# Rotary tables scaled once per layer, projection results copied out by ScalarE, rotary products on VectorE; earlier norm squares and first score blocks set wider apart, in a two-layer fp32 trunk

## The chip, the core and the metric

The kernel runs on one core of one Trainium2 chip. The metric is the device time of one execution, in microseconds (us). Five engines work side by side, each with its own queue that it runs in order: PE (TensorE, matmuls and transposes), DVE (VectorE), ACT (ScalarE), POOL (GpSimd) and SP (SyncE, which here only starts transfers).

## The reference, cut to what matters

512 tokens, model width 2048, two layers. Of one layer:

```python
h = rms_norm(x, pre_norm_g[l])                       # x * rsqrt(mean(x*x) + eps) * g
proj = einsum('bsd,de->bse', h, w_in[l])             # 2048 -> 6656 columns
rq, rk, rv, rg, dq, dk, dv, dg, lx, lg = split(proj) # 768 x4, 512 x4, 768 x2
ret  = rms_norm(retention(rope(rq), rope(rk), rv)) * silu(rg)       # 6 heads of 128
diff = rms_norm(diff_attention(rope(dq), rope(dk), dv)) * silu(dg)  # 4 heads, two softmaxes each
lru  = rg_lru(lx) * silu(lg)                         # convolution, two gates, a scan over time
y = einsum('bse,ed->bsd', concat([ret, diff, lru]), w_out[l])
x = x + rms_norm(y, post_norm_g[l])

def rope(x, positions, inv_freq):
    ang = positions[..., None] * inv_freq
    cos, sin = cos(ang)[:, :, None, :], sin(ang)[:, :, None, :]
    x1, x2 = split(x, 2, axis=-1)
    return concatenate([x1 * cos - x2 * sin, x2 * cos + x1 * sin], axis=-1)
```

All in fp32. The factor rsqrt(mean(x*x) + eps), below rstd, is one number for each token. The kernel leaves it out of the matmul's input and multiplies it into the results of the projection.

## The kernel before, in words

**The matmuls.** A layer is a list of passes: 13 over the input projection (512 columns each), then 5 over the output projection. A pass sums 16 blocks of 128 rows of the contraction into four PSUM banks, the tiles `big`. For fp32 accuracy each product is three matmuls on a high and a low part (`whi`, `wlo` of the weights, `hhi`, `hlo` or `mhi`, `mlo` of the activations), all on line L208. So a pass is 192 matmuls of 128x512. In this text a place in the program is counted in these "big" matmuls: the passes of layer 0 begin at 0 (dv), 192 (dq), 384 (dk), 576, 768, 960 (lx and lg), 1152, 1344, 1536 (rq and rk), 1728, 1920, 2112 (rv and rg), 2304 (dg) and from 2496 on the output projection; layer 1 begins at 3264.

**The weights.** They come in chunks of two row blocks (24 matmuls). SP loads a chunk into `raw`, ACT copies it to `whi` (L163), DVE subtracts to get `wlo` (L164). Three buffers of each: `whi` of a chunk may be written when PE has ended the chunk three before it, and PE needs it two chunks later.

**The end of a pass.** The last chunks are swept bank by bank, so that the banks finish 12 matmuls apart, and each is emptied (by the function `evac` of its pass) while the next goes on. The next pass begins with bank 0 and comes to bank b after 6·b matmuls.

**Side work.** All else (norm, rotary tables, rotation, attention, recurrent unit, retention) is written as Python generators in one queue, `side`. After every second group of 6 matmuls `pump` lets the generator at its head go on to its next `yield`; so a `yield` is 12 matmuls wide. PE runs what a generator issues between the big matmuls. A scheduler sets the order on each engine from the order in which instructions are issued and their priorities (`high_priority(HP)` moves the weight splits and the emptying of banks ahead); SP's order is as written.

**What the change touches.** `start_norm` (layer 0) squares the 16 tiles of x on ACT (L905) into tiles `xsq`, sums them on DVE and POOL (L907), and lets PE sum over partitions (`ssx`, L915, 16 matmuls with a single output column). `layer_rstd` makes rstd of it and spreads it to a tile `rsb`, 128x512, the factor of each token on every partition (PE transposes on L375). `tables` makes `cos_r`, `sin_r` (retention) and `cos_d`, `sin_d` (attention), once for both layers. `evac_rope` empties a bank of a rotary pass (dq, dk, rq, rk: five passes, 20 banks in each layer) by a DVE multiplication with `rsb` (L439) into `qk` and queues `rope`; that makes the crosswise sine products on DVE (L399 and L400, halves of 64 partitions; L404, quarters of 32, into `rt`), the cosine product on POOL (L401, L405) and the sum on POOL or DVE (L406). `stack` lays out high and low parts for the attention scores: ACT casts (L425, L426), and for keys POOL copies (L427, L428). `diff_attention` runs 16 units (4 query blocks i by 4 heads): scores on PE (`sc`, L462 and L463), row maximum on DVE (L465, L468), exponentials on ACT (`pr`, L471), then one unit later transposes on PE (`wT`, L485) and their copy on ACT (L487), and two units later the product with the values (`acc`, L495). `evac_lx` (L635) and `evac_lg` (L640, then a sigmoid on ACT, L642, and a product on POOL, L643) empty the banks of the recurrent unit; `evac_rvg` those of rv on DVE and ACT by turns (L740, L738). `silu_gate` (L535) is the sigmoid of the other gates. Most tiles of 128x512 come from one pool of 77 buffers, `up`, through `U(name)`: a new tile waits until the last reader of the tile that it replaces is done.

Of the kernel before, what the change touches and what calls it, by code (L numbers as in the profile page):

```python
# [13 lines left out]
F32 = mybir.dt.float32  # L14
# [3 lines left out]
AF = mybir.ActivationFunctionType  # L18
ALU = mybir.AluOpType
# [4 lines left out]
P = 128  # L24
# [13 lines left out]
WBUFS = 3  # L38
NWARM = 9
NPOOL = 4  # L40
LEAD, SLEAD, RLEAD = 4, 8, 6
DEFER = 3
HP = 300
XLEAD = {0: 0, 1: 1, 2: 2, 4: 3, 5: 4, 6: 5}
# [51 lines left out]
def tile_hybrid_trunk(ctx, tc, x, xt, pos, ppar, lamqk, w_in, gw, w_out, postg, cp, cm, out):  # L96
    nc = tc.nc
    V, A, G, T = nc.vector, nc.scalar, nc.gpsimd, nc.tensor

    ctx.enter_context(tc.manual_schedule(engines={mybir.EngineType.SP}))  # L100
    const = ctx.enter_context(tc.tile_pool(name="const", bufs=1))
# [14 lines left out]
    def U(s, dt=F32):  # L116
        return up.tile([P, S], dt, tag="u", name=nm(s))
# [5 lines left out]
    def SM(s):  # L123
        return pm.tile([P, S], F32, tag="sm", name=nm(s))
# [49 lines left out]
    side = deque()  # L174
# [59 lines left out]
    cos_r = const.tile([P, S], F32, name="cos_r")  # L234
    sin_r = const.tile([P, S], F32, name="sin_r")
# [130 lines left out]
    def layer_rstd(st):  # L366
        ss = tiny("ss", NT)
        V.tensor_reduce(ss, ssx, op=ALU.add, axis=AX.X)
        rsqrt_mean(rstd, ss, DM, NT)
        yield  # L370
        ps = SM("rsb")
        for tb in range(NT):
            rb = tp.tile([P, P], F32, tag="rb", name=nm("rb"), bufs=2)
            V.tensor_copy(rb, rstd[:, tb:tb + 1].to_broadcast([P, P]))
            T.transpose(ps[:, tb * P:(tb + 1) * P], rb, ident)  # L375
        st["rsb"] = U("rsb")
        V.tensor_copy(st["rsb"], ps)
        yield
# [15 lines left out]

    def rope(st, raw, dst, key, kind):
        yield from wait_ready()
        t2 = U("rt2")
        if kind == "ret":
            V.tensor_tensor(t2[64:128, :], raw[0:64, :], sin_r[0:64, :], op=ALU.mult)  # L399
            V.tensor_tensor(t2[0:64, :], raw[64:128, :], sin_r[64:128, :], op=ALU.mult)  # L400
            G.tensor_tensor(raw, raw, cos_r, op=ALU.mult)  # L401
        else:
            for a, b in ((0, 32), (32, 0), (64, 96), (96, 64)):
                V.tensor_tensor(t2[b:b + 32, :], raw[a:a + 32, :], sin_d[a:a + 32, :], op=ALU.mult)  # L404
            G.tensor_tensor(raw, raw, cos_d, op=ALU.mult)  # L405
        (G if kind == 'ret' else V).tensor_tensor(raw, raw, t2, op=ALU.add)  # L406
# [8 lines left out]
    def stack(st, nat, h, kind):  # L415
        lo_, hi_ = slice(0, 64), slice(64, 128)
        s0, s1 = U("st", F32R), U("st", F32R)
        if kind == "dq":
            A.copy(s0[lo_, :], nat[lo_, :])
            A.copy(s1[hi_, :], nat[hi_, :])  # L420
            V.tensor_tensor(s0[hi_, :], nat[lo_, :], s0[lo_, :], op=ALU.subtract)
            V.tensor_tensor(s1[lo_, :], nat[hi_, :], s1[hi_, :], op=ALU.subtract)
            st["dqs"][h] = (s0, s1)
        else:
            A.copy(s0[lo_, :], nat[lo_, :])  # L425
            A.copy(s1[hi_, :], nat[hi_, :])  # L426
            G.tensor_scalar(s0[hi_, :], nat[lo_, :], 1.0, 0.0, op0=ALU.mult, op1=ALU.add)  # L427
            G.tensor_scalar(s1[lo_, :], nat[hi_, :], 1.0, 0.0, op0=ALU.mult, op1=ALU.add)  # L428
            k0, k1 = U("kl", F32R), U("kl", F32R)
            G.memset(k0[hi_, :].bitcast(F32), 0.0)  # L430
            G.memset(k1[lo_, :].bitcast(F32), 0.0)
            V.tensor_tensor(k0[lo_, :], nat[lo_, :], s0[lo_, :], op=ALU.subtract)
            V.tensor_tensor(k1[hi_, :], nat[hi_, :], s1[hi_, :], op=ALU.subtract)
            st["dks"][h] = (s0, s1, k0, k1)
        yield

    def evac_rope(st, ps, dst, key, kind):
        raw = U("qk")
        V.tensor_tensor(raw, ps, st["rsb"], op=ALU.mult)  # L439
        side.append(rope(st, raw, dst, key, kind))  # L440


    def diff_attention(l, st):
# [46 lines left out]
        def stage_c(i, h):  # L490
# [6 lines left out]
            if h == DIFF_H - 1:  # L497
# [14 lines left out]
                V.tensor_tensor(o3, o3, f[:, :, None].to_broadcast([P, DIFF_H, P]), op=ALU.mult)  # L512
                st["dod"][i] = o

        for n in range(len(units) + 2):
            if n < len(units):
                stage_a(*units[n])
            if 0 <= n - 1 < len(units):
                stage_b(*units[n - 1])
            if 0 <= n - 2 < len(units):  # L520
                stage_c(*units[n - 2])
            yield
            if units[min(n, 15)][0] >= 2:
# [291 lines left out]

    def new_state():
        return {k: {} for k in ("h", "dq", "dk", "dqs", "dks", "dv", "dg", "lx", "lg", "lh", "rq", "rk", "rv", "rg", "ro",
                                "mix", "y", "ry", "xr", "pg")}

    states = [new_state() for _ in range(DEPTH)]  # L820
    for l in range(DEPTH - 1):
# [5 lines left out]
    for l in range(DEPTH):  # L827
        st = states[l]
# [70 lines left out]
    def start_norm():  # L899
        nc.sync.dma_start(cmt, cm)  # L900
        acc = {}
        for k in range(NK):
            j = int(k % NPOOL == 1)
            sq = U("xsq")
            A.activation(sq, xts[k], AF.Square)  # L905
            if j in acc:
                (V, G)[j].tensor_tensor(acc[j], acc[j], sq, op=ALU.add)  # L907
            else:
                acc[j] = sq
            if k % 2:  # L910
                yield
        ps = SM("ssx")
        for tb in range(NT):
            for j in range(2):
                T.matmul(ps[:, tb:tb + 1], lhsT=acc[j][:, tb * P:(tb + 1) * P], rhs=ones,  # L915
                         start=(j == 0), stop=(j == 1))
# [133 lines left out]
```

## Time and profile before

| what | value |
|---|---|
| time, median of 3 runs | 1665.0 us (1664.53 to 1665.46) |
| profiled execution: its own time | 1666.37 us |
| profiled execution: span from first to last instruction | 1664.4 us, so 1.97 us lie around it |
| mean granted TensorE clock | 0.993 |
| PE waits in the table of waits, sum of its 14 rows | 21.3 us |
| weight splits, 287 full chunks: ACT cast, DVE subtraction | 1052 ns, 1290 ns each |

How to read it: PE's busy time is a share of the span; what remains is waits. Times beside a line are the mean of one instruction. A matmul's own duration (390 ns) is longer than the distance to the next (0.2275 us at full clock), as they overlap. In a window's row, PEclk is the clock that PE was granted there, 1.00 being full.

### The profile page before, as it was taken

The page shows a single profiled execution, that of the slowest core. Times are in us where ns is not written, and L with a number is a line of the kernel's source. Part 1 is how long each engine was busy: PE and PEld are TensorE (multiplying, and loading weights), DVE is VectorE, ACT ScalarE, POOL GpSimd, SP SyncE. Part 2 cuts the span into 40 slices and gives each one's busy share as a digit, 9 for nine tenths or more (in the row PEclk, how much of TensorE's full clock was granted, in tenths as well). Part 3 has the DMA queues.
Part 4 walks back from the last instruction along what each step waited for, and adds up shares of the span by engine and source line. Part 5 has one row for each costly group of instructions (what it writes and reads, how often), then busy time and mean ns, then how long its engine had stood idle before and what let it go on. Part 6 is the DMA issues. An engine that isn't in the chain of part 4 may idle for free. (4 is left out here: it accounts for less than half of the span.)

```text
span 1664.4 us, 19440 instructions
## 1 busy us (share of the span) xinstructions
PE 1634.2 (98%) x7541; PEld 1349.5 (81%) x7541; DVE 928.7 (56%) x1474; ACT 626.0 (38%) x966; POOL 259.1 (16%) x216
## 2 busy tenths in 40 slices
PE   9999899999999999999999998999999999999997
PEld 7788788787877888888888887888888888888886
DVE  6767765665674444322772776664677544442336
ACT  6232345457212323222662224346541222332233
POOL 0011400111261110000110131003035301100003
PEclk9999999999999999999999999999999999999999
DMA  7233222232322222344643222222323322223635
GB/s 258 79 92 101 89 64 84 89 96 76 102 76 77 76 89 83 107 146 158 222 159 100 89 89 77 76 84 83 92 86 102 101 73 77 91 96 108 196 124 199
DMA packets 54747, 177.50 MB, mean 107 GB/s; under 512 B 6656, under 2 KB 7680, under 8 KB 54656
## 3 DMA queue, kind: packets, MB, share of 16 engines
q1 hardware_dynamic: 52592, 169.94, 32.2%
q0 software_dynamic: 1920, 6.29, 1.0%
q8 instruction: 59, 0.97, 0.2%
q14 instruction: 32, 0.26, 0.1%
q10 hardware_dynamic: 144, 0.04, 0.0%
HBM read 167.86 MB, written 8.39 MB: 106 GB/s over the span
## 5 line engine op out<-in xcount | busy, mean ns | idle before, releaser
L164 DVE TENSOR_TENSOR wlo<-raw,whi 128x1024 fp32r<-128x1024 f32 (+1 forms) x289 | 370.5, 1286 | 426.7 <-ACT whi L163 412.8
L163 ACT CAST whi<-raw 128x1024 fp32r<-128x1024 f32 (+1 forms) x289 | 302.6, 1049 | 630.2 <-PE big L208 549.1
L208 PE MATMUL big<-hhi,whi 128*128 128x512 f32 x1024 | 402.9, 394 | 1.5 <-DVE lx L635 1.5
L208 PE MATMUL big<-hhi,wlo 128*128 128x512 f32 x1024 | 400.6, 391 | 1.6 <-DVE wlo L164 1.6
L208 PE MATMUL big<-hlo,whi 128*128 128x512 f32 x1024 | 400.0, 391 | 0.0
L208 PE MATMUL big<-whi,hhi 128*128 128x512 f32 x640 | 255.3, 401 | 3.7 <-ACT rv L738 2.6
L208 PE MATMUL big<-wlo,hhi 128*128 128x512 f32 x640 | 252.0, 395 | 2.7 <-DVE wlo L164 2.7
L208 PE MATMUL big<-whi,hlo 128*128 128x512 f32 x640 | 251.6, 393 | 0.0
L208 PEld LDWEIGHTS big<-hhi,wlo 128*128 128x128 f32 x1024 | 192.9, 188 | 42.5 <-DVE wlo L164 2.0
L208 PEld LDWEIGHTS big<-hhi,whi 128*128 128x128 f32 x1024 | 193.0, 188 | 41.7 <-DVE lx L635 2.0
L208 PEld LDWEIGHTS big<-hlo,whi 128*128 128x128 f32 x1024 | 193.0, 189 | 38.8
L208 PE MATMUL big<-wlo,mhi 128*128 128x512 f32 x512 | 199.5, 390 | 0.6 <-DVE wlo L164 0.6
L208 PE MATMUL big<-whi,mlo 128*128 128x512 f32 x512 | 199.8, 390 | 0.0
L208 PE MATMUL big<-whi,mhi 128*128 128x512 f32 x512 | 199.8, 390 | 0.0
L208 PEld LDWEIGHTS big<-wlo,hhi 128*128 128x128 f32 x640 | 121.5, 190 | 29.4 <-DVE wlo L164 3.1
L208 PEld LDWEIGHTS big<-whi,hhi 128*128 128x128 f32 x640 | 121.5, 190 | 28.3 <-ACT rv L738 3.0
L208 PEld LDWEIGHTS big<-whi,hlo 128*128 128x128 f32 x640 | 121.6, 190 | 24.2
L208 PEld LDWEIGHTS big<-wlo,mhi 128*128 128x128 f32 x512 | 96.1, 188 | 21.2 <-DVE wlo L164 1.5
L208 PEld LDWEIGHTS big<-whi,mlo 128*128 128x128 f32 x512 | 96.2, 188 | 19.7
L208 PEld LDWEIGHTS big<-whi,mhi 128*128 128x128 f32 x512 | 96.1, 188 | 19.6
L773 POOL TENSOR_TENSOR ry<-sy,mhalf 128x1 f32<-128x1 f32 x8 | 4.7, 585 | 406.7 <-DVE sy L771 406.7
L471 ACT ACTIVATE pr<-sc,mx 128x128 f32<-128x128 f32 (+3 forms) x64 | 33.3, 525 | 75.7 <-DVE mx L468 75.6
(212 smaller groups left out, 1530.0 us busy)
## 6 DMA issues: line engine op xcount, KB each, us to landing
raw<-in_w_in SPq DMA_DIRECT2D x207, 512.0 KB, 3.6
raw<-in_w_out SPq DMA_DIRECT2D x80, 512.0 KB, 3.5
xT<-in_xt SPq DMA_DIRECT2D x16, 256.0 KB, 6.6
xr<-in_x SPq DMA_DIRECT2D x16, 256.0 KB, 5.5
xs<-y POOLq DMA_DIRECT2D x16, 256.0 KB, 3.5
xr<-xs SPq DMA_DIRECT2D x16, 256.0 KB, 5.5
pg<-in_postg SPq DMA_DIRECT2D x8, 256.0 KB, 3.9
out<-y POOLq DMA_DIRECT2D x8, 256.0 KB, 4.5
```

Source lines behind the costliest of these rows:

```text
L163: last_copy[0] = A.copy(hi[:, a:b, :], raw[:, a:b, :])
L164: V.tensor_tensor(lo[:, a:b, :], raw[:, a:b, :], hi[:, a:b, :], op=ALU.subtract)
L208: T.matmul(ps[b], lhsT=lhsT, rhs=rhs, start=(cnt[b] == 0), stop=(cnt[b] == total - 1))
L471: A.activation(p[:, :n], sc[c][:, :n], AF.Exp, bias=mx[:, c:c + 1], scale=0.125, accum_out=sums[:, h:h + 1])
L773: G.tensor_tensor(st["ry"][tb], ms, mhalf[:, :1], op=ALU.pow)
```

## The change

1. `scale_tables` is new: once in each layer, after rstd is known, DVE makes four tables `cos·rsb`, `sin·rsb` (tiles of the pool `up`, given back when the last of 8 or 20 rotations has been issued).
2. `evac_rope` becomes an ACT copy. `rope` uses the scaled tables, and all its products and sums are on DVE. Of 20 sums a layer, 12 go from POOL to DVE, as do all 20 cosine products.
3. In `stack` the two POOL copies of a key become ACT casts.
4. `start_norm`: squares and sums get the priority of the weight splits, and two `yield`s stand between them and `ssx`.
5. `diff_attention` begins with an exponential of a 128x1 tile and one `yield`; and the first four turns of its loop get a second `yield` (24 matmuls apart where they were 12 apart).

```diff
+    def scale_tables(st):
+        yield from wait_ready()
+        for name, table in (("cos_d", cos_d), ("sin_d", sin_d), ("cos_r", cos_r), ("sin_r", sin_r)):
+            st[name] = U(name)
+            V.tensor_tensor(st[name], table, st["rsb"], op=ALU.mult)
+            if name[0] == "s":
+                yield
+        st["turned"] = 0
     def rope(st, raw, dst, key, kind):
-        yield from wait_ready()
+        while st["turned"] is None:
+            yield
         t2 = U("rt2")
         if kind == "ret":
-            V.tensor_tensor(t2[64:128, :], raw[0:64, :], sin_r[0:64, :], op=ALU.mult)
-            V.tensor_tensor(t2[0:64, :], raw[64:128, :], sin_r[64:128, :], op=ALU.mult)
-            G.tensor_tensor(raw, raw, cos_r, op=ALU.mult)
+            cos, sin = st["cos_r"], st["sin_r"]
+            swaps, w = ((0, 64), (64, 0)), 64
         else:
-            for a, b in ((0, 32), (32, 0), (64, 96), (96, 64)):
-                V.tensor_tensor(t2[b:b + 32, :], raw[a:a + 32, :], sin_d[a:a + 32, :], op=ALU.mult)
-            G.tensor_tensor(raw, raw, cos_d, op=ALU.mult)
-        (G if kind == 'ret' else V).tensor_tensor(raw, raw, t2, op=ALU.add)
+            cos, sin = st["cos_d"], st["sin_d"]
+            swaps, w = ((0, 32), (32, 0), (64, 96), (96, 64)), 32
+        for a, b in swaps:
+            V.tensor_tensor(t2[b:b + w, :], raw[a:a + w, :], sin[a:a + w, :], op=ALU.mult)
+            if w == 32 and a == 32:
+                yield
+        V.tensor_tensor(raw, raw, cos, op=ALU.mult)
+        V.tensor_tensor(raw, raw, t2, op=ALU.add)
...
-            G.tensor_scalar(s0[hi_, :], nat[lo_, :], 1.0, 0.0, op0=ALU.mult, op1=ALU.add)
-            G.tensor_scalar(s1[lo_, :], nat[hi_, :], 1.0, 0.0, op0=ALU.mult, op1=ALU.add)
+            A.copy(s0[hi_, :], nat[lo_, :])
+            A.copy(s1[lo_, :], nat[hi_, :])
...
     def evac_rope(st, ps, dst, key, kind):
         raw = U("qk")
-        V.tensor_tensor(raw, ps, st["rsb"], op=ALU.mult)
+        A.copy(raw, ps)
         side.append(rope(st, raw, dst, key, kind))
...
+        A.activation(ones2, ones, AF.Exp)
+        yield
         for n in range(len(units) + 2):
...
-            if units[min(n, 15)][0] >= 2:
+            if n < 4 or units[min(n, 15)][0] >= 2:
                 yield
...
             sq = U("xsq")
-            A.activation(sq, xts[k], AF.Square)
-            if j in acc:
-                (V, G)[j].tensor_tensor(acc[j], acc[j], sq, op=ALU.add)
-            else:
-                acc[j] = sq
+            with tc.high_priority(HP):
+                A.activation(sq, xts[k], AF.Square)
+                if j in acc:
+                    (V, G)[j].tensor_tensor(acc[j], acc[j], sq, op=ALU.add)
+                else:
+                    acc[j] = sq
             if k % 2:
                 yield
+        yield from lead(NLEAD)
         ps = SM("ssx")
```

Three places show what moves. First DVE in the first pass, where the squares' sums (`xsq`) and the weights' subtractions (`wlo`) stand. Before:

```order
L907 TENSOR_TENSOR xsq_268<-xsq_268,xsq_287 128x512
L164 TENSOR_TENSOR wlo_400<-raw_398,whi_399 128x1024
L907 TENSOR_TENSOR xsq_268<-xsq_268,xsq_302 128x512
L164 TENSOR_TENSOR wlo_461<-raw_459,whi_460 128x1024
L907 TENSOR_TENSOR xsq_268<-xsq_268,xsq_320 128x512
L164 TENSOR_TENSOR wlo_491<-raw_489,whi_490 128x1024
L907 TENSOR_TENSOR xsq_268<-xsq_268,xsq_323 128x512
```

After:

```order
L931 TENSOR_TENSOR xsq_269<-xsq_269,xsq_375 128x512
L931 TENSOR_TENSOR xsq_269<-xsq_269,xsq_393 128x512
L931 TENSOR_TENSOR xsq_269<-xsq_269,xsq_396 128x512
L165 TENSOR_TENSOR wlo_401<-raw_399,whi_400 128x1024
L165 TENSOR_TENSOR wlo_431<-raw_429,whi_430 128x1024
L165 TENSOR_TENSOR wlo_492<-raw_490,whi_491 128x1024
L942 COPY ssx<-ssx_447 128x4
```

Before, nine of the eleven sums stand behind a weight chunk that waits for PE, seven of them behind the third one shown; now all eleven stand ahead of the first of the three chunks. `ssx` on PE moves from big matmul 179 to 144.

Second, DVE at the turn from the last rq/rk pass to the first rv pass of layer 0, where `rt` are the sine products of a rotation and `rv` the emptying of the first rv bank. Before (the cosine product and the sum of each `qk` are on POOL):

```order
L164 TENSOR_TENSOR wlo_3706<-raw_3704,whi_3705 128x1024
L400 TENSOR_TENSOR rt_712_3792<-qk_3334,sin_r 64x512
L399 TENSOR_TENSOR rt_716_3827<-qk_3354,sin_r 64x512
L400 TENSOR_TENSOR rt_716_3827<-qk_3354,sin_r 64x512
L399 TENSOR_TENSOR rt_720_3862<-qk_3611,sin_r 64x512
L400 TENSOR_TENSOR rt_720_3862<-qk_3611,sin_r 64x512
L164 TENSOR_TENSOR wlo_3741<-raw_3739,whi_3740 128x1024
L164 TENSOR_TENSOR wlo_3776<-raw_3774,whi_3775 128x1024
```

After (here all of a rotation is on DVE):

```order
L417 TENSOR_TENSOR rt_716_3844<-qk_2822,sin_r_1137 64x512 x2
L165 TENSOR_TENSOR wlo_3736<-raw_3734,whi_3735 128x1024
L420 TENSOR_TENSOR qk_2822<-qk_2822,cos_r_1135 128x512
L421 TENSOR_TENSOR qk_2822<-qk_2822,rt_716_3844 128x512
L165 TENSOR_TENSOR wlo_3776<-raw_3774,whi_3775 128x1024
L165 TENSOR_TENSOR wlo_3816<-raw_3814,whi_3815 128x1024
L165 TENSOR_TENSOR wlo_3851<-raw_3849,whi_3850 128x1024
L763 TENSOR_SCALAR rv_3873<-big_3618,rstd 128x128
```

Where five sine products stood between two weight subtractions, four products and sums of one rotation stand around one. POOL has no rotary work left in this stretch.

Third, ACT at big matmuls 1104 to 1194 of layer 0, the last lx/lg pass and the attention's third query block. `lgs` is the sigmoid of a bank, `pr` the exponentials of a score block, `wT` the copy of its transpose. After:

```order
L665 ACT_TABLE_LOAD
L665 ACTIVATE lgs_2342<-lg_2340 128x512
L665 ACTIVATE lgs_2359<-lg_2357 128x512
L491 ACT_TABLE_LOAD
L491 ACTIVATE pr_2372,s_399_2217<-sc_2363,mx_2362 128x384
L491 ACTIVATE pr_2374,s_400_2218<-sc_2366,mx_2362 128x384
L164 CAST whi_2329<-raw_2328 128x1024
L507 COPY wT_2384<-wT_2380 128x384
L164 CAST whi_2456<-raw_2455 128x1024
L665 ACT_TABLE_LOAD
L665 ACTIVATE lgs_2404<-lg_2402 128x512
L665 ACTIVATE lgs_2421<-lg_2419 128x512
```

Before, the four sigmoids of this pass:

```order
L642 ACT_TABLE_LOAD
L642 ACTIVATE lgs_2550<-lg_2548 128x512
L642 ACTIVATE lgs_2567<-lg_2565 128x512
L567 CAST gwh_2571<-gwr_2570 96x384
L163 CAST whi_2537<-raw_2536 128x1024
L567 CAST gwh_2577<-gwr_2576 96x384
L163 CAST whi_2645<-raw_2644 128x1024
L642 ACTIVATE lgs_2596<-lg_2594 128x512
L584 CAST xh_2606<-xc_2601 128x512
L585 CAST x4h_2599<-xc_2601 32x512
L642 ACTIVATE lgs_2626<-lg_2624 128x512
```

Before, the attention of layer 0 has issued its last scores at big matmul 1044, so the four sigmoids come after it with one table load. After, the scores run from 936 to 1248, and sigmoids and exponentials take turns on ACT, with a table load at each turn; as the tiles of both come from `up`, more of its 77 buffers are in use at once there. In the whole program ACT's order has 32 table loads before and 32 after. The two new exponentials of a 128x1 tile, one for each layer, both stand at ACT's start, ahead of the sine table's load, and the load ahead of a layer's first `pr` still stands there.

More of the change, by code (lines that the diff above doesn't have):

```diff
@@ L40 @@
 NPOOL = 4
-LEAD, SLEAD, RLEAD = 4, 8, 6
+LEAD, SLEAD, RLEAD, NLEAD = 4, 8, 6, 2
 DEFER = 3
@@ L144, in tile_hybrid_trunk @@
     A.activation(ones, ones, AF.Identity)
+    ones2 = const.tile([P, 1], F32, name="ones2")
     passes = []
@@ L392, in wait_ready @@
             yield
+    def scale_tables(st):
[6 more added lines that the diff above has]
+        st["turned"] = 0
     def rope(st, raw, dst, key, kind):
-        yield from wait_ready()
+        while st["turned"] is None:
+            yield
         t2 = U("rt2")
         if kind == "ret":
-            V.tensor_tensor(t2[64:128, :], raw[0:64, :], sin_r[0:64, :], op=ALU.mult)
-            V.tensor_tensor(t2[0:64, :], raw[64:128, :], sin_r[64:128, :], op=ALU.mult)
-            G.tensor_tensor(raw, raw, cos_r, op=ALU.mult)
-        else:
-            for a, b in ((0, 32), (32, 0), (64, 96), (96, 64)):
-                V.tensor_tensor(t2[b:b + 32, :], raw[a:a + 32, :], sin_d[a:a + 32, :], op=ALU.mult)
-            G.tensor_tensor(raw, raw, cos_d, op=ALU.mult)
-        (G if kind == 'ret' else V).tensor_tensor(raw, raw, t2, op=ALU.add)
+            cos, sin = st["cos_r"], st["sin_r"]
+            swaps, w = ((0, 64), (64, 0)), 64
+        else:
+            cos, sin = st["cos_d"], st["sin_d"]
[6 more added lines that the diff above has]
+        V.tensor_tensor(raw, raw, t2, op=ALU.add)
+        st["turned"] += 1
+        if st["turned"] == 8:
+            del st["cos_d"], st["sin_d"]
+        elif st["turned"] == 20:
+            del st["cos_r"], st["sin_r"]
         if kind == "ret":
@@ L817, in new_state @@
         return {k: {} for k in ("h", "dq", "dk", "dqs", "dks", "dv", "dg", "lx", "lg", "lh", "rq", "rk", "rv", "rg", "ro",
-                                "mix", "y", "ry", "xr", "pg")}
+                                "mix", "y", "ry", "xr", "pg")} | {"turned": None}
     states = [new_state() for _ in range(DEPTH)]
@@ L937, in tile_hybrid_trunk @@
         if l == 0:
-            side.append(chain(start_norm(), lead(LEAD), tables(), layer_params(0), layer_params(1), ready()))
+            side.append(chain(start_norm(), lead(LEAD), tables(), layer_params(0), layer_params(1), ready(), scale_tables(st)))
         else:
-            side.append(chain(lead(RLEAD), layer_rstd(st)))
+            side.append(chain(lead(RLEAD), layer_rstd(st), scale_tables(st)))
         for i, (p, tasks) in enumerate(layer_passes[l]):
```

## The prediction

> **What bounds the kernel now.** I read the busy table first, then PE's waits, then the places where PE waits long, on the timeline, and the granted clock there.
>
> ```profile
> PE 1634.2 (98%) x7541; PEld 1349.5 (81%) x7541; DVE 928.7 (56%) x1474; ACT 626.0 (38%) x966; POOL 259.1 (16%) x216
> ```
>
> PE is the bound. The change removes no matmul, so it can only win what PE loses: waits, and matmuls at a lower clock. The waits (engine, line, what is waited for: us in total, times, longest):
>
> ```profile
> PE sc L462 <- ACT pr L471: 5.2, 3, 2.8
> PE big L208 <- DVE wlo L164: 4.9, 4, 2.7
> PE big L208 <- ACT rv L738: 2.6, 1, 2.6
> PE big L208 <- DVE lx L635: 1.5, 1, 1.5
> PE ssx L915 <- DVE xsq L907: 1.4, 1, 1.4
> PE wT L485 <- ACT whi L163: 0.7, 1, 0.7
> PE gate L599 <- DVE xl L587: 0.4, 1, 0.4
> ```
>
> These are few, and nearly all the long ones lie where the change works. The timeline gives their place (start, duration, in brackets the idle time before):
>
> ```profile
> 48.78 2.99 PE L915 MATMUL ssx<-ones,xsq 128*128 128x1 f32 x16 [1.44 <-DVE xsq L907]
> 180.58 0.50 PE L208 MATMUL big<-hhi,wlo 128*128 128x512 f32 x1 [1.60 <-DVE wlo L164]
> 199.59 0.33 PE L462 MATMUL sc<-st,st 128*128 128x128 f32 x1 [1.73 <-ACT pr L471]
> 473.36 6.61 DVE L164 TENSOR_TENSOR wlo<-raw,whi 128x1024 fp32r<-128x1024 f32 x3
> 475.59 0.50 PE L208 MATMUL big<-wlo,hhi 128*128 128x512 f32 x1 [2.70 <-DVE wlo L164]
> 505.46 0.50 PE L208 MATMUL big<-whi,hhi 128*128 128x512 f32 x1 [2.59 <-ACT rv L738]
> 1002.52 1.28 ACT L471 ACT_TABLE_LOAD   x1
> 1002.57 1.23 DVE L164 TENSOR_TENSOR wlo<-raw,whi 128x1024 fp32r<-128x1024 f32 x1
> 1005.05 0.39 PE L462 MATMUL sc<-st,st 128*128 128x128 f32 x1 [2.80 <-ACT pr L471]
> ```
>
> And the clock in the windows behind four of them (columns: busy time and count of PE, PEld, DVE, ACT, POOL, then PEclk, DMA share, GB/s):
>
> ```profile
> 49.00:57.00 8.00, 8.00 (x32) 6.76 (x32) 2.87 (x9) 1.99 (x3) 1.03 (x1) 0.57 0.01 2
> 475.00:481.00 6.00, 5.41 (x17) 4.29 (x18) 4.97 (x3) 0.00 (x0) 3.81 (x2) 0.72 0.56 165
> 505.00:512.00 7.00, 6.54 (x25) 5.34 (x26) 1.24 (x2) 1.41 (x2) 0.00 (x0) 0.76 0.52 160
> 1004.00:1012.00 8.00, 6.27 (x17) 4.95 (x18) 3.62 (x17) 2.70 (x10) 0.00 (x0) 0.57 0.41 131
> ```
>
> One minus the clock, times the width, is time lost: 8·0.43 = 3.44, 6·0.28 = 1.68, 7·0.24 = 1.68, 8·0.43 = 3.44 us. So a wait of 2.6 us or more costs another 1.7 or 3.4 us at half clock; at the waits of 1.6 and 1.73 us I saw no loss of clock. The Trainium skill ("TensorE: Matmul & The Clock Gate", Part 1, "What's actually happening") gives a free-running activity window of 3413 ns, and losses in units of 1.7 us, half of that, agree. Its rule in "Why this matters for your kernels" (avoid idle gaps over about 3 us) does not: here 2.59 us already cost a window, so the measurement decides. By the rule, rival 1 below would cost its waits alone and come out 3.4 us lower; the forecast stays the same by both.
>
> **The parts.** The rows for the prices:
>
> ```profile
> L401 POOL TENSOR_TENSOR qk<-qk,cos_r 128x512 f32<-128x512 f32 x24 | 44.0, 1834 | 95.6 <-DVE rt L400 92.8 <-PE big L208 2.8
> L406 POOL TENSOR_TENSOR qk<-qk,rt 128x512 f32<-128x512 f32 x24 | 42.6, 1776 | 1.9
> L405 POOL TENSOR_TENSOR qk<-qk,cos_d 128x512 f32<-128x512 f32 x16 | 23.6, 1473 | 169.7 <-DVE rt L404 167.4 <-issue 2.3
> L643 POOL TENSOR_TENSOR lgs<-lgs,lg 128x512 f32<-128x512 f32 x12 | 17.4, 1454 | 78.3 <-ACT lgs L642 78.3
> L404 DVE TENSOR_TENSOR rt<-qk,sin_d 32x512 f32<-32x512 f32 x64 | 43.7, 683 | 1.2
> L400 DVE TENSOR_TENSOR rt<-qk,sin_r 64x512 f32<-64x512 f32 x24 | 31.0, 1293 | 0.4
> L439 DVE TENSOR_TENSOR qk<-big,rsb 128x512 f32<-128x512 f32 x40 | 27.4, 688 | 22.7 <-PE big L208 22.5
> L406 DVE TENSOR_TENSOR qk<-qk,rt 128x512 f32<-128x512 f32 x16 | 11.1, 691 | 17.4 <-POOL qk L405 17.4
> L640 DVE TENSOR_TENSOR lg<-big,rsb 128x512 f32<-128x512 f32 x12 | 8.3, 688 | 9.7 <-PE big L208 9.7
> L907 DVE TENSOR_TENSOR xsq<-xsq,xsq 128x512 f32<-128x512 f32 x11 | 10.5, 955 | 0.9 <-ACT xsq L905 0.2
> L487 ACT COPY wT<-wT 128x512 f32<-128x512 f32 x8 | 4.7, 585 | 3.1 <-PE wT L485 3.1
> L425 ACT CAST st<-qk 64x512 fp32r<-64x512 f32 x8 | 5.0, 621 | 42.1 <-DVE qk L406 42.1
> L642 ACT ACTIVATE lgs<-lg 128x512 f32<-128x512 f32 x12 | 7.6, 633 | 11.0 <-DVE lg L640 10.9
> L471 ACT ACT_TABLE_LOAD x5 | 6.4, 1283 | 3.4 <-DVE mx L468 3.4
> ```
>
> *Loads of the engines.* A DVE product takes 0.69 us beside an idle POOL (L406) and 1.29 beside a multiplying one (L400). DVE gives up 40 evacuations (27.4 us); it takes on 24 products and 24 sums of retention, 16 cosine products and 8 table products, 72·0.69 = 49.7; and the 48 sine halves, freed of POOL, should fall from 1.29 (one half's row) towards 0.69, a gain of 14 us for that half alone and less for the other. So DVE's total stays about the same, while POOL loses 44.0 + 42.6 + 23.6 = 110 us and its key copies. ACT gains 40·0.585 + 16·0.621 = 33 us of 1664. No engine becomes full on average; what counts is the order at the places below.
>
> *Start (squares).* Two rows more:
>
> ```profile
> 26.32 2.18 ACT L905 ACTIVATE xsq<-xT 128x512 f32<-128x512 f32 x4
> 40.18 4.80 ACT L905 ACTIVATE xsq<-xT 128x512 f32<-128x512 f32 x9
> ```
>
> Sixteen squares in a row from 26.32 at 4.80/9 = 0.533 end near 34.9; eleven sums at 0.955 from 28 end by 38.5 at worst. `ssx` moves up 35 matmuls: 48.78 − 1.44 − 35·0.2275 = 39.4. So its wait of 1.44 goes. The split of the next chunk now stands behind the sums (38.5 + 1.29 = 39.8 at worst), which the 2 to 3 us of `ssx` itself cover. The clock: of the 3.44 us lost about 0.6 fell on `ssx`, so 2.8 count. But `ssx`, 16 matmuls of one column, may well drop the clock for a window again without any wait: between a gain of 2.8 and none I take one window kept, 1.1. Start: 2.5 (1.4 to 4.2).
>
> *First score blocks.* Twelve matmuls are 2.73 us; the chain from scores over maximum, exponentials (behind a table load and weight splits) back to a free score tile did not fit, and fits in 24 matmuls, 5.46 us. In layer 0 the waits 1.60, 1.53 (the row of `lx` above) and 1.73 go: 4.9. In layer 1: 2.80, then 0.7 (`wT` on `whi`), and about 2.9 of the 3.44 us of clock: 6.4. The table load itself stays; in the new order it stands behind a `whi` and nothing else, so ACT loads while PE is still ahead. The early 128x1 exponential does nothing for it, as it stands at ACT's start and the sine table follows: 0. One `yield`: 0, 12 matmuls of other work.
>
> *Retention rotations.* At 473 three subtractions took 6.61 us, 2.2 each, beside POOL; without POOL 1.23 (the row at 1002.57). In the new order four chunks' time there (21.8 us) holds some 19 us of DVE work at 0.69. So 2.70 + 1.7 = 4.4 go. At 505, between the first and the last `rv` on DVE, stand 10 rotary instructions, 2 subtractions and 8 `rv` of 0.35: 6.9 + 2.5 + 2.8 = 12.2 us against 3·2.73 + 18·0.2275 = 12.3 until the next pass wants bank 3. So 2.59 + 1.7 = 4.3 go, by a hair; if the hair fails, 0.
>
> *ACT copies.* A bank is emptied in 0.585 instead of 0.688: 0 on the path, unless ACT is late (rival 3).
>
> *New costs.* (a) Layer 0, 1125 to 1200: the attention now overlaps the last lx/lg pass, and `up` is used to its last buffer. By the orders, a tile of `up` was reused no sooner than 24 big matmuls after its last reader; now eleven are reused within 0 to 5. An `lg` waits for the transpose that reads the tile before it; the next `lg` for evacuation, sigmoid and POOL product of its forerunner, 0.69 + 0.63 + 1.45 (+ 1.28 for a table load); the next `pr` for that. Behind the waiting `lg` on DVE stand the weight subtraction and the row maxima; behind the waiting `pr` on ACT a `whi`. Laid beside 0.2275 a matmul, PE waits about 0.3 + 0.75 + 0.2 + 0.2 + 0.75 + 0.5 = 2.7 us (0 to 9). None reaches a clock drop. (b) Gates, layer 1: they move into the end of a pass and four stand within 3 matmuls of one another; with three score tiles and 0.63 us for a sigmoid, 1.5 us. (c) Small waits as in the rows of 0.4 to 0.7 above, dealt anew: 1.0. Together 5.2 (0 to 12).
>
> **Sum.** 2.5 + 4.9 + 6.4 + 4.4 + 4.3 = 22.5 won, 5.2 given back: 17.3. The profiled execution took 1666.37 (span 1664.4 and 1.97 around it), 1.4 above the median of 1665.0; from the profile 1649.1, from the median 1647.7. I say **1648 us**.
>
> **Rivals.**
>
> 1. *Short of buffers.* If table loads fall into chain (a), bank 3 and `wT` wait 2.0 instead of 0.75 each, and two windows run at half clock: 2.5 + 3.4 more, **1654**. For it: two sigmoid and two exponential loads in 50 matmuls. Against: a load can run while ACT waits for its input.
> 2. *VectorE late at the retention rotations.* More of a rotation stands on DVE, ahead of the splits. If the hair at 505 and the place at 473 fail, 4.3 and 4.4 stay: **1656**. For it: 12.2 against 12.3. Against: POOL, which had stretched each instruction there, is gone.
> 3. *ScalarE late with banks: slower.* The evacuation of rq and rk leaves DVE, which waited only for PE there (L439: 22.5 of 22.7 us idle), and queues on ACT behind the recurrent unit's sigmoids, exponentials and their loads of 1.28 us. Three passes in two layers: if a bank is late by w, PE waits w, with 1.7 of clock from about 2.5 us on. It decides at w = 17.3/6 = 2.9; at 2.6 with one window, 6·4.3 = 26, less 17.3: **1674**. Against: copies have the splits' priority, and my hand-laid slack is 1.3 us in the tightest pass.
> 4. *The waits only move.* The first scores meet the `lx`, `lg` evacuations at 936 and 4008; if PE waits there as before (4.9 + 6.4), and one more pair of windows drops, **1663**.
> 5. *All gains, no new cost*: 1665.0 − 22.5 − 1.7 = **1641**.
>
> **Chances.** The forecast's case (1643 to 1653) 0.58, rival 1 0.14, rival 2 0.11, rival 3 0.08, rival 4 0.05, rival 5 0.04. 0.2%, 3.3 us, is what a measurement tells from no change: faster 0.58 + 0.14 + 0.11 + 0.04 = 0.87, same 0.05 (rival 4), slower 0.08 (rival 3). The range runs from rival 5 past rival 2, 1641 to 1659, leaving out the others and a little beyond.
>
> **What would show it.** Right: no wait at `ssx`; no `sc` waiting for `pr` over 1 us; L417 and L420 near 0.69 us and `wlo` near 1.23 by the rv passes; PEclk 1.00 there; short waits of `big` and `wT` on `lg` and `pr` some 17 us long in the last lx/lg pass of layer 0. Wrong: `big` waiting for `qk` on ACT (rival 3), PEclk of 0.5 in that lg pass (rival 1), a wait on `rv` left (rival 2).

## The result, and the profile after

The changed kernel takes 1642.1 us (median of 4 runs, 1641.68 to 1643.2) against 1665.2 us for the kernel before on the same chip: ratio 0.9859, 95% interval 0.9848 to 0.9871. That is 23 us faster, where 17 were forecast; 1642.1 lies inside the range, near its low end. The profiled execution spans 1640.1 us where the one before spanned 1664.4, and its mean clock is 0.999 instead of 0.993. The ratios and intervals, here and below, leave out one far slower execution each of `only_spread` (1808 us) and `no_early_exp` (6946 us).

The busy row of the page, to be read against the one of before:

```profile
PE 1623.5 (99%) x7541; PEld 1342.6 (82%) x7541; DVE 902.8 (55%) x1506; ACT 656.5 (40%) x1024; POOL 133.1 (8%) x136
```

PE has the same 7541 matmuls. ACT took on 30.5 us and POOL gave up 126, as priced; DVE did 32 instructions more in 26 us less. The table of PE's waits:

```profile
PE warm L950 <- POOL warm L947: 1.4, 1, 1.4
PE big L209 <- DVE wlo L165: 1.2, 3, 0.5
PE wT L505 <- ACT wT L507: 1.1, 1, 1.1
PE sc L482 <- ACT pr L491: 0.8, 2, 0.4
PE hT L828 <- DVE hlo L836: 0.8, 1, 0.8
PE big L209 <- ACT whi L164: 0.7, 1, 0.7
PE wT L505 <- ACT whi L164: 0.5, 1, 0.5
PE big L209 <- DVE lg L663: 0.5, 1, 0.5
```

No wait over 1.1 us is left after the start. The row for `rv` and the one for `ssx` are gone, `wlo` fell from 4.9 to 1.2, `sc` on `pr` from 5.2 to 0.8. The groups on which the prices rested (mean in ns before the second bar):

```profile
L165 DVE TENSOR_TENSOR wlo<-raw,whi 128x1024 fp32r<-128x1024 f32 x287 | 353.1, 1234 | 447.6 <-ACT whi L164 441.3 <-DMA xr<-xs 4.2 <-PE hT L828 0.9
L417 DVE TENSOR_TENSOR rt<-qk,sin_r 64x512 f32<-64x512 f32 x48 | 32.9, 686 | 1.2
L420 DVE TENSOR_TENSOR qk<-qk,cos_r 128x512 f32<-128x512 f32 x24 | 16.5, 687 | 0.3
L459 ACT COPY qk<-big 128x512 f32<-128x512 f32 x40 | 23.3, 583 | 40.7 <-PE big L209 40.6
```

A sine product fell from 1293 and 1079 (the means of its two halves) to 686 ns, the weight subtraction from 1290 to 1234; a copy on ACT waits for PE and for next to nothing else (40.6 of 40.7 us). The trace of the kernel before holds the same comparison within itself: of its 48 sine products, the 16 beside which POOL did no product, sum or copy took 0.69 us each, the other 32 took 0.68 to 1.69. An emptying of a bank (L439) took 0.69 us in both cases, so not every DVE instruction is slowed.

To find where the time came from, I took from each timeline the first big matmul, and the first one of the passes at 192, 1728, 2496, 3264, 3456, 4992 and 5760 (the operands change there). The time between them, in us, one profiled execution each (layer 1's first pass and the output passes have no column):

| kernel | 0 to 192 | 192 to 1728 | 1728 to 2496 | 3456 to 4992 | 4992 to 5760 |
|---|---|---|---|---|---|
| what lies there | first pass, norm | layer 0: attention, recurrent unit | layer 0: rv, rg, dg | layer 1: attention, recurrent unit | layer 1: rv, rg, dg |
| before | 50.9 | 393.2 | 208.6 | 392.2 | 199.5 |
| changed | 47.0 | 387.0 | 199.4 | 386.4 | 199.4 |
| rotation alone | 50.1 | 385.6 | 199.6 | 386.7 | 199.4 |
| rotation alone, short | 49.4 | 388.4 | 199.4 | 387.4 | 199.4 |
| spreading alone | 49.7 | 392.3 | 213.0 | 386.4 | 205.4 |
| changed, start as before | 50.8 | 386.4 | 199.4 | 386.3 | 199.4 |
| changed, no spreading | 47.4 | 387.4 | 199.4 | 389.8 | 199.4 |
| changed, retention products on POOL | 48.2 | 387.1 | 207.7 | 386.3 | 209.1 |
| changed, attention's POOL work back | 48.2 | 389.0 | 199.4 | 386.3 | 199.4 |

Differences of before and changed: 3.9 + 6.2 + 9.2 + 5.8, some 25, less 1.5 in the output passes and the end, plus 0.6 ahead of the first matmul: 24.3, the difference of the spans.

### The profile page after: what moved, and what is told of

It reads as the page before. It is cut to its first block, busy times and chain, and to the rows that moved or that the text cites. A ratio compares the mean times of both kernels' runs of the same rounds, so it can differ in the third digit from the quotient of the medians.

```text
span 1640.1 us, 19400 instructions
## 1 busy us (share of the span) xinstructions
PE 1623.5 (99%) x7541; PEld 1342.6 (82%) x7541; DVE 902.8 (55%) x1506; ACT 656.5 (40%) x1024; POOL 133.1 (8%) x136
## 4 chain that ended last, share of the span: by engine, by line
PE 93%; DVE 3%; issue 2%; ACT 1%; POOL 1%; DMA 0%; DVEq 0%; POOLq 0%; ACTq 0%
PE big L209 86%; PE gate L622 1%; DVE wlo L165 1%; PE acc L515 1%; PE ro L709 1%; PE rs L684 1%; PE ro L712 0%; PE kv L698 0%; PE sc L483 0%; PE sc L482 0%; PE wT L505 0%; ACT whi L164 0%; PE hT L828 0%; DVE y L820 0%; PE rT L739 0%
## 5 line engine op out<-in xcount | busy, mean ns | idle before, releaser
L165 DVE TENSOR_TENSOR wlo<-raw,whi 128x1024 fp32r<-128x1024 f32 (+1 forms) x289 | 354.5, 1230 | 447.8 <-ACT whi L164 441.3
L209 PEld LDWEIGHTS big<-hhi,whi 128*128 128x128 f32 x1024 | 192.4, 188 | 40.6 <-DVE lg L663 0.9
L417 DVE TENSOR_TENSOR rt<-qk,sin_d 32x512 f32<-32x512 f32 x64 | 43.7, 683 | 3.5 <-ACT qk L459 2.5
```

The lines of the kernel that those rows point to most:

```text
L165: V.tensor_tensor(lo[:, a:b, :], raw[:, a:b, :], hi[:, a:b, :], op=ALU.subtract)
L209: T.matmul(ps[b], lhsT=lhsT, rhs=rhs, start=(cnt[b] == 0), stop=(cnt[b] == total - 1))
L417: V.tensor_tensor(t2[b:b + w, :], raw[a:a + w, :], sin[a:a + w, :], op=ALU.mult)
```

## The experiments

Each is compared by its ratio to the kernel before, run beside it on the same chip; the changed kernel's is 0.9859 (0.9848 to 0.9871).

**The rotation alone** (`only_rotation`): the changed kernel with the start, the exponential and the spacing of before.

```diff
-            with tc.high_priority(HP):
-                A.activation(sq, xts[k], AF.Square)
...
-        yield from lead(NLEAD)
...
-        A.activation(ones2, ones, AF.Exp)
-        yield
...
-            if n < 4 or units[min(n, 15)][0] >= 2:
+            if units[min(n, 15)][0] >= 2:
```

> The kernel before with the scaled tables, the ScalarE copies and casts and the VectorE products alone: start, exponential and spacing of the first scores as before. Theory A: only the stretch of the rv passes gains, 9.2 us (to big matmul 2496: 19.95 - 10.77), and a little in the attention of layer 0: about 1655. Theory B (POOL's products are also behind the waits at the first scores): 1665.2 - 9.2 - 10 = 1646.

1642.99 us, ratio 0.9865 (0.9849 to 0.9881). This part alone brings the whole gain, within what the runs can tell. Its waits:

```profile
PE ssx L936 <- DVE xsq L928: 1.4, 1, 1.4
PE big L209 <- DVE wlo L165: 1.0, 2, 0.5
PE sc L482 <- ACT pr L491: 0.8, 2, 0.7
```

No score waits longer than 0.7 us, though the first ones still stand 12 matmuls apart. Theory A, by which only the rv stretch gains (1655), falls. Theory B fits, and the time lies 3 us below even its 1646. The place of the scores has changed too, though: the new yields move the first ones from 780 to 900 in layer 0 and from 3948 to 3996 in layer 1. The fourth experiment separates the two.

**The spreading alone** (`only_spread`): the kernel before with `if n < 4 or ...`.

```diff
-            if units[min(n, 15)][0] >= 2:
+            if n < 4 or units[min(n, 15)][0] >= 2:
```

> The kernel before with the first four score blocks 24 matmuls apart and nothing else. Theory A: waits of sc on pr go in both layers, 1665.2 - 1.7 - 6.4 = 1657. Theory B (VectorE beside POOL is behind those waits): the waits get smaller but stay, 1661 to 1664.

1668.66 us, ratio 1.0015 (1.0006 to 1.0024): no gain, and both theories had one. In the table, layer 1's attention does fall from 392.2 to 386.4, layer 0's barely, and both rv stretches get longer. In layer 0 the waits of 1.6 us at `wlo` and 1.5 at `lx` stay, and in place of the 1.73 at a score stand 1.8 at `wT` and 1.4 at a later score. PE's rows in the rv stretches:

```profile
472.56 0.50 PE L208 MATMUL big<-wlo,hhi 128*128 128x512 f32 x1 [2.70 <-DVE wlo L164]
...
500.27 0.50 PE L208 MATMUL big<-whi,hhi 128*128 128x512 f32 x1 [1.77 <-ACT rv L738]
506.25 0.80 PE L208 MATMUL big<-whi,hhi 128*128 128x512 f32 x1 [4.33 <-ACT rv L738]
...
1300.26 0.79 PE L208 MATMUL big<-wlo,hhi 128*128 128x512 f32 x1 [2.84 <-DVE wlo L164]
```

An attention that lasts longer pushes the retention rotations, next in the queue of side work, against the rv passes, in layer 1 too, where before they had been done in time (the last sine product of layer 1 began at 1297.2 there and at 1318.4 here). What is won at the scores is lost there.

**Retention's products back on POOL** (`pool_products`): 24 cosine products and 24 sums, nothing else.

```diff
-        V.tensor_tensor(raw, raw, cos, op=ALU.mult)
-        V.tensor_tensor(raw, raw, t2, op=ALU.add)
+        E = G if kind == "ret" else V
+        E.tensor_tensor(raw, raw, cos, op=ALU.mult)
+        E.tensor_tensor(raw, raw, t2, op=ALU.add)
```

> The changed kernel with the cosine product and the sum of the 24 retention rotations back on POOL (scaled tables and ScalarE copies kept). Theory A (VectorE stretched by POOL's products is behind the waits at the rv passes): the 9.2 us of that stretch come back in good part, wlo near 2 us there, 1648 to 1651. Theory B (the gain there came from taking the 24 evacuations of rq and rk off VectorE, and from the order): under 2 us, 1642 to 1644.

1659.86 us, ratio 0.9968 (0.9956 to 0.9981): three quarters of the gain are gone, 17.8 us, twice what theory A said, since layer 1's rv stretch loses as much as layer 0's. The sine products of DVE, and PE's waits:

```profile
L417 DVE TENSOR_TENSOR rt<-qk,sin_r 64x512 f32<-64x512 f32 x48 | 55.3, 1153 | 1.2
```

```profile
489.86 0.50 PE L209 MATMUL big<-whi,hhi 128*128 128x512 f32 x1 [1.77 <-ACT rv L762]
495.84 0.50 PE L209 MATMUL big<-whi,hhi 128*128 128x512 f32 x1 [4.32 <-ACT rv L762]
...
1290.30 0.80 PE L209 MATMUL big<-wlo,hhi 128*128 128x512 f32 x1 [4.14 <-DVE wlo L165]
...
1320.93 0.50 PE L209 MATMUL big<-whi,hhi 128*128 128x512 f32 x1 [2.59 <-ACT rv L762]
```

The same sine products take 1153 instead of 686 ns. DVE's rows, from one emptying of an rv bank (`rv`) to another:

```profile
480.55 0.35 DVE L764 TENSOR_SCALAR rv<-big,rstd 128x128 f32<-128x128 f32 x1
...
482.64 4.69 DVE L417 TENSOR_TENSOR rt<-qk,sin_r 64x512 f32<-64x512 f32 x3
...
490.73 2.19 DVE L165 TENSOR_TENSOR wlo<-raw,whi 128x1024 fp32r<-128x1024 f32 x1
...
493.11 2.02 DVE L165 TENSOR_TENSOR wlo<-raw,whi 128x1024 fp32r<-128x1024 f32 x1
495.05 0.34 DVE L764 TENSOR_SCALAR rv<-big,rstd 128x128 f32<-128x128 f32 x1
```

These are six emptyings, six sine products and two subtractions, with no wait between them. They took 14.8 us; at 0.35, 0.686 and 1.234 us they would take 8.7. The 6.1 us between are as much as the two waits of 1.77 and 4.32 on `rv`. So the slower pace explains these waits without any change of order. In the window from 480 to 500 us the engines' busy time and count read (PE, PEld, DVE, ACT, POOL; first this kernel, then the changed one):

```profile
480.00:500.00 20.00, 13.91 (x53) 10.77 (x52) 19.56 (x19) 5.12 (x9) 17.47 (x11) 0.92 0.17 52
```

```profile
480.00:500.00 20.00, 20.00 (x90) 16.57 (x89) 19.53 (x30) 5.99 (x10) 0.00 (x0) 1.00 0.27 82
```

DVE is full in both, with 19 instructions done beside POOL and 30 without it. POOL's 11 instructions would have been about 7.6 us of work on DVE (11·0.69). DVE's own 18 that begin there from 480.5 us on took 19.5 us, where 11.4 is their time at the means above. So handing the work to POOL freed nothing in this stretch.

**The rotation alone, without the yields inside it** (`short_rope`), so that layer 1's first scores stand at 3948, 12 apart, as in the kernel before (layer 0's at 804, where they were at 780).

```diff
-            if w == 32 and a == 32:
-                yield
```

> The kernel with the rotation's change alone (scaled tables, ScalarE copies, all products on VectorE), without the yield inside a rotation: the first scores of layer 1 stand at 3948 and 12 apart, where they were in the kernel before; layer 0 begins at 804 instead of 780. Theory A (the first scores were late because of the work beside POOL): no wait of sc on pr over 1 us, 3456 to 4992 in 386 to 387 us, whole time 1643. Theory B (they were late because they stood too early and too close, and the rotation's yields had moved them): the 2.8 us wait and two windows at half clock come back in layer 1, 392 us, and 1.7 us in layer 0; whole time 1649 to 1651.

1646.01 us, ratio 0.9889 (0.9872 to 0.9905), between the theories. In layer 1 the place and distance of the scores are those of before, and the long wait does not come back:

```profile
PE sc L480 <- ACT pr L489: 2.3, 4, 0.7
PE wT L503 <- ACT whi L164: 1.7, 2, 0.8
```

The way from layer 1's first scores to their row maximum shows why. In this kernel:

```profile
982.70 0.27 PE L480 MATMUL sc<-st,st 128*128 128x128 f32 x1
...
985.30 0.29 DVE L483 CUSTOM_DVE_ANT_0 sc<-sc,cmt 128x128 f32<-128x128 f32 x1
```

and in the kernel before:

```profile
998.91 0.27 PE L462 MATMUL sc<-st,st 128*128 128x128 f32 x1
...
999.45 0.69 DVE L406 TENSOR_TENSOR qk<-qk,rt 128x512 f32<-128x512 f32 x1 [1.18 <-POOL qk L405]
...
1001.54 0.99 DVE L433 TENSOR_TENSOR kl<-qk,st 64x512 fp32r<-64x512 f32 x1
...
1003.71 0.29 DVE L465 CUSTOM_DVE_ANT_0 sc<-sc,cmt 128x128 f32<-128x128 f32 x1
```

2.6 us here, 4.8 there: DVE was still finishing the last key's rotation, for whose cosine product it had waited on POOL, when the first scores were ready. Theory A holds for the long waits, not for its 1643: short waits are left, and the attention stretches are 2.8 + 0.7 us longer than in the kernel with the yields. By the medians these yields are worth some 3 us too, but the two intervals overlap.

**No spreading** (`no_spread`), in the changed kernel.

```diff
-            if n < 4 or units[min(n, 15)][0] >= 2:
+            if units[min(n, 15)][0] >= 2:
```

> The changed kernel with the first four score blocks 12 matmuls apart again. Theory A (spreading is what frees the first score blocks): the waits of sc on pr of 1.7 us in layer 0 and 2.8 us with two windows at half clock in layer 1 come back, 6 to 9 us, 1648 to 1651. Theory B (the first score blocks had been late because rotations beside POOL kept VectorE busy; with POOL idle they fit in 12 matmuls): 1642 to 1644, no wait of sc over 1 us.

1646.18 us, ratio 0.9882 (0.9868 to 0.9895), between the theories. No score waits over 0.42 us, so theory B holds for the mechanism. Of the 3.4 us lost in layer 1, 1.9 are at two gates that now meet their casts; the clock is full there, and I cannot place all of the rest:

```profile
1118.66 0.47 PE L622 MATMUL gate<-xh,gwh 96*96 96x512 f32 x1 [1.28 <-ACT xh L607]
1119.75 0.47 PE L622 MATMUL gate<-xl,gwh 96*96 96x512 f32 x1 [0.62 <-DVE xl L610]
```

The rotation alone has no spreading either, stands 12 matmuls earlier in layer 1, and needs 386.7 us there. So this is a matter of where the side work falls, not of the scores' distance.

**The start as before** (`old_squares`), in the changed kernel; the edit is the first part of that of the rotation alone.

> The changed kernel with the start as before: squares and sums without priority, no two yields ahead of ssx. Theory A (the parts add up, and the start is worth what the time to big matmul 192 shows, 57.31 - 52.79 = 4.5 us, of which 0.6 lies ahead of the first big matmul): ssx waits about 1.4 us again, two windows run at half clock, 1642.1 + 3.9 = 1646.0. Theory B (the start was worth only the 2.5 us of the prediction): 1644.6.

1644.74 us, ratio 0.9875 (0.9858 to 0.9891). By the medians the start is worth 2.6 us, but the intervals overlap and do not tell 2.5 from 3.9. In the profile `ssx` waits again, and behind it one window's worth of clock is lost, 1.7 us, not two:

```profile
48.65 1.95 PE L938 MATMUL ssx<-ones,xsq 128*128 128x1 f32 x16 [1.44 <-DVE xsq L930]
```

**One-column matmuls for three times as long** (`ssx_x3`).

```diff
+        ps3 = SM("ssx3")
+        for r in (1, 2):
+            for tb in range(NT):
+                for j in range(2):
+                    T.matmul(ps3[:, tb + 4 * r:tb + 4 * r + 1], lhsT=acc[j][:, tb * P:(tb + 1) * P], rhs=ones,
+                             start=(j == 0), stop=(j == 1))
```

> The changed kernel with the 16 one-column matmuls of ssx issued two times more into an unused score tile, so that PE works on one-column matmuls for 5.9 us instead of 1.95. Theory A (matmuls of one column do not count as work for the clock, as the prediction feared): a window at half clock for at least 1.7 us, 1642.1 + 3.9 + 1.7 = 1647.7 or more. Theory B (they count; only the wait before them had dropped the clock): PEclk 1.00 throughout, 1642.1 + 3.9 = 1646.0.

1646.92 us, ratio 0.9889 (0.9875 to 0.9903). The time lies between the theories (1646.0 and 1647.7), so the trace has to tell. The matmuls follow one another with no wait, and in the rows behind them (PEclk third from the end) the clock falls:

```profile
38.94 1.95 PE L940 MATMUL ssx<-ones,xsq 128*128 128x1 f32 x16
40.74 4.01 PE L946 MATMUL ssx<-ones,xsq 128*128 128x1 f32 x32
```

```profile
44.00:46.00 2.00, 2.00 (x8) 1.75 (x8) 0.27 (x2) 0.00 (x0) 0.00 (x0) 0.50 0.89 271
46.00:48.00 2.00, 2.00 (x7) 1.59 (x6) 0.00 (x0) 0.00 (x0) 0.00 (x0) 0.65 0.83 286
```

2·0.50 + 2·0.35 = 1.7 us lost. Theory B falls: the clock dropped with no wait ahead of it. It can do so behind 1.95 us of one-column matmuls already: of eight profiles with the new start, the usual 16 and no wait at `ssx`, three lost 1.7 us of clock behind it (the 0 to 192 stretch then takes 48.2 to 48.7) and five lost none (47.0 to 48.2). So one profile with 48 that lost it does not show that more of these matmuls make the loss surer; the direction of theory A is right, its price for a longer run of them stays open.

**Three more parts.** The banks of the rotary passes copied by DVE (`dve_copy`):

```diff
-        A.copy(raw, ps)
+        V.tensor_copy(raw, ps)
```

> The changed kernel with the banks of the rotary passes copied out by VectorE instead of ScalarE. Theory A (the engine of the copy is not on the path; VectorE has room without POOL): 1642 within 1.5 us. Theory B (the evacuations on VectorE were part of what made weight splits late): 3 us or more longer, with big waiting for wlo or for qk at the ends of the rotary passes.

1642.28 us, ratio 0.9862 (0.9846 to 0.9877): theory A; the engine of the copy is not on the path. The exponential left out (`no_early_exp`):

```diff
-        A.activation(ones2, ones, AF.Exp)
         yield
```

> The changed kernel without the 128x1 exponential ahead of the attention (its yield kept). Theory A (it stands at the start of ScalarE's order and loads nothing for the scores): within 0.5 us of 1642.1, the same number of table loads. Theory B (it moves the table load off the path): 1.3 us or more longer.

1641.57 us, ratio 0.9855 (0.984 to 0.987): theory A; no effect of it can be seen. The attention's cosine products and key copies back on POOL (`pool_diff`):

```diff
-        V.tensor_tensor(raw, raw, cos, op=ALU.mult)
+        (V if kind == "ret" else G).tensor_tensor(raw, raw, cos, op=ALU.mult)
...
-            A.copy(s0[hi_, :], nat[lo_, :])
-            A.copy(s1[lo_, :], nat[hi_, :])
+            G.tensor_scalar(s0[hi_, :], nat[lo_, :], 1.0, 0.0, op0=ALU.mult, op1=ALU.add)
+            G.tensor_scalar(s1[lo_, :], nat[hi_, :], 1.0, 0.0, op0=ALU.mult, op1=ALU.add)
```

> The changed kernel with the cosine products of the attention's rotations and the key copies back on POOL (16 and 16 instructions); order of PE as in the changed kernel. Theory A (with the first scores at 936 and 4008 the attention's POOL work has no part in any wait; only the 24 retention rotations' products did harm): within 1.5 us of 1642. Theory B (they did harm too): waits of sc, lx or wlo of 1.5 us and more return at the first scores, 1646 or more.

1642.94 us, ratio 0.9868 (0.9853 to 0.9883): theory A; layer 0's attention takes 2 us more by the table, and no first score waits long. With the first scores at 936 and 4008 the rotations are done long before (in layer 1, DVE's last rotary row ends some 10 us ahead of the first score). So POOL's products made the first scores wait only where these followed closely behind the last rotation; and in layer 1 of the spreading alone, at the old place but 24 apart, that wait was gone as well.

**Two tries for a faster kernel.** Retention's scaled tables made later (`late_tables`), two buffers fewer in use:

```diff
-        for name, table in (("cos_d", cos_d), ("sin_d", sin_d), ("cos_r", cos_r), ("sin_r", sin_r)):
+        for name, table in (("cos_d", cos_d), ("sin_d", sin_d)):
...
-            if name[0] == "s":
-                yield
+        yield
...
+    def scale_late(st):
+        for name, table in (("cos_r", cos_r), ("sin_r", sin_r)):
...
+            if i == 6:
+                side.append(scale_late(st))
             run_pass(p)
```

> The changed kernel with the two scaled tables of retention made only when the first rq pass begins, so that two more of the 77 buffers are free while the attention overlaps the last lx/lg pass of layer 0. Theory A (shortage of buffers is behind the waits of wT and big of 1.1 and 0.5 us there): they go or halve, 192 to 1728 about 1.4 us shorter, 1640.7. Theory B (table loads and VectorE's order are behind them): the same waits, 1642.

1641.01 us, ratio 0.9857 (0.9843 to 0.9872). The two waits that theory A named, of `wT` on `wT` and of `big` on `lg`, are gone from the table of waits, which would fit the shortage. But the edit also takes one yield away, so that layer 0's first scores stand 12 matmuls earlier (at 924) and ACT's table loads fall elsewhere; the shortage is not shown. The attention stretch is only 0.5 us shorter (386.5), and the rv passes are 0.7 longer. And the attention where it stood with the rotation alone, with the new start (`earlier_attention`):

```diff
-LEAD, SLEAD, RLEAD, NLEAD = 4, 8, 6, 2
+LEAD, SLEAD, RLEAD, NLEAD = 2, 8, 6, 2
...
-        A.activation(ones2, ones, AF.Exp)
-        yield
...
-            if n < 4 or units[min(n, 15)][0] >= 2:
+            if units[min(n, 15)][0] >= 2:
```

> The changed kernel without spreading, without the early exponential and its yield, and with two yields fewer ahead of the tables, so that the attention stands where it did with the rotation's change alone (first scores at 900 and 3996), but the squares' part is kept. Theory A (segments add up: the start in 47.0 us, 192 to 1728 in 385.6): 1640.5, 1.5 to 2 us faster than the changed kernel. Theory B (the spreading is needed once the start is shorter): 1643 or more, with waits of sc or wT near 900 or 3996.

1641.36 us, ratio 0.9858 (0.9844 to 0.9873). Its attention stretches are those of the rotation alone (385.6 and 386.7), as theory A said, but its profile lost one window behind `ssx`. Neither beats the changed kernel beyond the interval.

## Why the prediction was right, and where its sizes and one of its reasons were wrong

*Start.* Forecast 2.5; the two profiles give 3.9, the medians of `old_squares` 2.6. The wait went as worked out (39.4 was forecast):

```profile
38.83 1.95 PE L940 MATMUL ssx<-ones,xsq 128*128 128x1 f32 x16
```

Three things were in that term: the wait, 1.44; the half clock; and `ssx` itself, 1.95 instead of 2.99. By the two profiles the step that was mis-sized is "I take one window kept", as the changed kernel's kept none. But that is chance: the kernel before lost two windows in its profile and the four other profiles with the old start one each, while of the eight with the new start three lost one. On average the stretch from 0 to 192 takes 50.2 us in the five and 47.8 in the eight. That is 2.4 apart, so the forecast was about right.

*First score blocks.* The step that failed is its reason: "the chain ... did not fit, and fits in 24 matmuls". I had seen the table load and the subtraction ahead of the maximum, and not that DVE came to them late because it had waited for POOL. In layer 1 either cure removes the long wait: spreading alone, as forecast, and the rotation without its inner yields, at the old place and the old distance. In layer 0 the reason is wrong: with spreading alone the waits of 1.6 at `wlo` and 1.5 at `lx` stay and the one at the score only moves, while they are gone wherever the rotation is changed. Neither run of the rotation alone keeps layer 0's old place exactly (900 and 804 for 780). After its new costs the forecast was 4.9 − 2.7 = 2.2 in layer 0 and 6.4 − 1.5 = 4.9 in layer 1; measured are 6.2 and 5.8. The waits went all the same because the change contains both cures; as far as the reason goes, that is luck.

*Retention rotations.* Forecast 4.4 + 4.3 = 8.7, measured 9.2; both waits went. The hair at bank 3 held, with no wait on `rv`: from the first to the last emptying on DVE stand nine rotary instructions, two subtractions and eight `rv`, in 11.2 us, where 12.2 was forecast and 12.3 was allowed. What I did not see: with the attention later, POOL's products would also have cost layer 1's rv stretch 9.7 us, so that moving them prevents a loss that the kernel before did not have.

*ACT copies, early exponential.* Priced at 0; `dve_copy` and `no_early_exp` differ from the changed kernel by 0.2 and 0.5 us, inside the intervals.

*New costs.* Forecast 5.2, some 2 measured in layer 0 and nearly none at layer 1's gates (0.25 us). Part of chain (a) is there, at the place described:

```profile
280.43 1.28 ACT L491 ACT_TABLE_LOAD   x1 [1.81 <-DVE mx L488]
...
284.22 0.48 ACT L507 COPY wT<-wT 128x384 f32<-128x384 f32 x1 [0.33 <-DVE pr L497]
...
284.76 0.55 PE L505 MATMUL wT<-cmt,pr 128*128 128x128 f32 x3 [1.12 <-ACT wT L507]
...
288.52 1.29 POOL L666 TENSOR_TENSOR lgs<-lgs,lg 128x512 f32<-128x512 f32 x1 [8.19 <-ACT lgs L665]
289.84 0.69 DVE L663 TENSOR_TENSOR lg<-big,rsb 128x512 f32<-128x512 f32 x1 [1.62 <-POOL lgs L666]
...
290.58 0.50 PE L209 MATMUL big<-hhi,whi 128*128 128x512 f32 x1 [0.48 <-DVE lg L663]
```

The new `lg` waits for POOL's product, as chain (a) has it, and PE 0.48 us for the `lg`. The 1.12 at `wT` has another source: the copy that PE waited for stood on ACT behind exponentials that had waited 1.81 us for the row maximum and then 1.28 for a table load, the condition of rival 1. With 0.39 at a score that is 2.0 instead of 2.7, with no loss of clock. The term (b) was mis-sized: the gates of layer 1 waited 0.25 us instead of 1.5. Why is not shown; I take it that ACT had come further than I had laid it.

*Rivals.* Of the rivals that cost time none came: no clock lost in the lg pass, no wait on `rv`, none on `qk`. Rival 5, all gains without new cost at 1641, was nearest, and 1642.1 lies just below the 1643 at which the forecast's case began. So the outcome lies nearest to what had been given a chance of 0.04, though new costs of some 2 us did come.

*The sum.* By spans 24.3 instead of 17.3. Of the 7 us, 1.4 are the start and 0.6 lie ahead of the first matmul (which begins between 5.2 and 8.5 us in the fourteen profiles), both in good part the chance of two executions; 4.0 are layer 0 from 192 to 1728 (6.2 instead of 4.9 − 2.7), 0.5 the rv passes, 0.9 layer 1 (5.8 instead of 6.4 − 1.5), less 0.5 elsewhere. Of layer 0's 4.0, the waits that the two traces show explain about 2.2: new ones of 2.0 instead of 2.7, and small ones of about 1.5 in the kernel before that I had not counted as gains. Another part is in how I read the rows: an idle time is counted from a matmul's modelled end, 0.39 us after its start, while the next could start after 0.2275, so each wait costs some 0.16 us more than its row says, with seven waits over 0.15 us there before and three after. What is left, about 1 us, I cannot place.

## What to carry to other kernels

Work that is handed to POOL to unload a vector engine that is half idle on average can slow that engine exactly where it is full; price it in the stretch where both run, by the mean of each kind of the neighbour's instructions with and without it, as some are slowed and others not. When two edits each remove the same wait, undoing one shows nothing: run each alone from the old kernel as well. And when side work runs in one queue, a yield more at its head moves all that follows against other ends of passes, so a local gain has to be looked for in the whole table of stretches.

## What the runs showed of the hardware that I had not expected

VectorE's products of 64x512 took 686 ns with POOL idle; with POOL's products they took 1079 and 1293 ns (means of the two halves, kernel before) and 1153 (all 48, `pool_products`), single ones up to 1.69 us. The weight subtraction of 128x1024 went from 1.22 to up to 2.3 us. The emptyings of banks, which read one of their inputs from PSUM, kept their time beside POOL: 0.69 us (L439, kernel before) and 0.35 us (L764, `pool_products`). PE can lose 1.7 us of clock behind one-column matmuls that it ran without any wait: in three profiles of eight after 1.95 us of them, and in the one profile with 6 us of them.
